# The transposes of both token tiles of an FFN chunk share one PSUM bank and are recorded in one loop

## The chip, the cores and the metric

The kernel runs on one NeuronCore of a Trainium2 chip. The metric is the device time of one execution in microseconds (us). A core has engines with queues of their own: TensorE (PE: matmuls and transposes; PEld: its weight loads, which overlap them), VectorE (DVE), ScalarE (ACT), GpSimd (POOL) and SyncE (SP, which issues the loads here). They run beside each other, each works its queue in order, and an instruction waits at the head of its queue until the semaphores that it names have been raised.

## The reference, cut to what matters

Two layers over 256 tokens of width 1024. Each layer is a feed-forward stage (FFN), a mixer (a state-space branch beside an attention branch) and a second FFN. Only the FFN is touched:

```
def swiglu(h, wi, wo):
    gate, up = jnp.split(h @ wi, 2, axis=-1)
    return (jax.nn.silu(gate) * up) @ wo

for l in range(DEPTH):
    x = x + 0.5 * swiglu(rms_norm(x, norm_ffn1[l]), ffn1_wi[l], ffn1_wo[l])
    ...                                     # the mixer
    x = x + 0.5 * swiglu(rms_norm(x, norm_ffn2[l]), ffn2_wi[l], ffn2_wo[l])
```

The inner width is 2816, so `wi` is 1024 x 5632 and `wo` 2816 x 1024.

## The kernel before

**Tiles.** The 256 tokens are two token tiles, t = 0 and 1, of 128. An FFN runs over 11 chunks c of 256 inner columns. In a chunk, `gemm` multiplies both tiles with 256 gate and 256 up columns of `wi` into two PSUM banks named `gu`. ACT computes the silu of the gate half (line 512), DVE multiplies it with the up half (line 513), which gives `act[t]`, 128 tokens x 256. To be multiplied with `wo` it has to stand with its inner columns on the partitions, so PE transposes it in two blocks of 128 x 128 (line 496) into a PSUM bank named `tr`, of which there are two, shared with all other transposes of the program.

**Split numbers.** Each product is formed from a high and a low part of both factors in three matmuls: line 381 (high x high), 382 (low of the first x high) and 383 (high x low), in `mm3`. So every factor has to be split: `split` (lines 347 to 349) copies the value to the short format on ACT (a cast, the high part) and then subtracts that from the value on DVE (the low part). Weights are split the same way when they have landed: `ffn_wi` and `w_in` with the gain of the norm on lines 169 (ACT, `whi`) and 170 (DVE, `wlo`), `ffn_wo` on line 349. There are four buffers of each for the split weights, so a weight split waits until PE has read the buffer for the last time.

**The product with `wo`** is formed one chunk late: `wo_mm(c - 1, t, i)` adds 128 inner columns of the chunk before to the PSUM banks `ya` (tile 0, two halves) and `yb` (tile 1). So in the loop stand: the matmuls of `gu` for chunk c, half of the `wo` matmuls for chunk c - 1, the transposes for chunk c, and the other half. At the last chunk no next one follows: `finish` (line 385 on) calls `part(0, 0)`, which multiplies the transposed tile 0 of that very chunk with `wo`, then the rest for tile 1. Behind `part(0, 0)` DVE adds the result to the residual `x` (line 391) and PE transposes `x` for the next stage (line 375).

**What sets the order.** The program is recorded in the order of the code, and a scheduler then gives each engine its queue, by a model of when operands are ready. `tc.issue_after(ins)` holds what is recorded in its block behind `ins`, for instructions of the same engine as `ins`. Tiles of a pool wait for the last reader of the buffer that they take. `k.bg` is side work of the mixer's preparation that is recorded between the chunks of the first FFN of each layer.

Of the kernel before, what the change touches and what calls it, by code (L numbers as in the profile page):

```python
# [11 lines left out]
ALU = mybir.AluOpType  # L12
# [67 lines left out]
class Model:  # L80
# [127 lines left out]
    def plan(k):  # L208
# [28 lines left out]
        for l in range(L):  # L237
            ffn(l, A['ffn1_wi'], A['ffn1_wo'], 0)
            cols(l, C_U)
            cols(l, C_KC, 384)  # L240
            cols(l, C_VS, 408)
            w1 = A['cmp_w1']
            for kv in range(2):
                for i in range(2):
                    k.add(bass.AP(tensor=w1.tensor, offset=w1.offset + ((l * 2 + kv) * 2048 + i * 1024) * 128,
                                  ap=[[128, 128], [128 * 128, 8], [1, 128]]), split=False)
            for c0 in (C_Q, C_GA, C_GA + 512, C_GB, C_GB + 512):
                cols(l, c0)
            for c in range(4):
                for i in range(2):  # L250
                    k.add(ap2(A['ssm_w_glu'], l, i * 256, 2, c * 256, D, 256))
            for c in range(2):
                for i in range(2):
                    w = A['nsa_w_up']
                    k.add(tuple(bass.AP(tensor=w.tensor, offset=w.offset + (l * 512 + g * 256 + i * 128) * D + c * 512,
                                        ap=[[D, 64], [64 * D, 2], [1, 512]]) for g in range(2)))
            for i in range(8):
                k.add(ap(A['w_out'], l, i * 128, 1, 0, D))
            ffn(l, A['ffn2_wi'], A['ffn2_wo'], 2)
# [219 lines left out]
    def ffn(k, hooks, sc, norm, order):  # L479
        nc = k.nc  # L480
        y = {}
        aT = {}

        def wo_mm(c, t, i, W, hs=(0, 1)):
            ah, al = aT[c, t]
            hi, lo = W
            for h in hs:
                cs = slice(h * 512, (h + 1) * 512)
                k.mm3(y[t, h], (ah[:, i], al[:, i]), (hi[:, cs], lo[:, cs]),
                      c == 0 and i == 0, c == NFF - 1 and i == 1)  # L490

        def transposes(c, act):
            for t in range(2):
                b = k.bank((128, 2, 128))
                for i in range(2):
                    nc.tensor.transpose(b[:, i], act[t][:, i * 128:(i + 1) * 128], k.id)  # L496
                hi = k.sb([128, 2, 128], "w1k", k.opt['n1'], F32R)
                lo = k.sb([128, 2, 128], "w1k", k.opt['n1'], F32R)
                k.split(b, hi, lo)
                aT[c, t] = (hi, lo)  # L500

        last = NFF - 1
        for c in range(NFF):
            ps = k.gemm(k.hstat, 8, 512, order if c == 0 else None, la=k.opt['LB'] if c == 0 else None)
            if c == 0:
                k.norms()
                r = k.rn
            act = []
            for t in range(2):
                sg = k.sb([128, 256], "w1k", k.opt['n1'])  # L510
                a = k.sb([128, 256], "w1k", k.opt['n1'])
                m = nc.scalar.activation(sg, ps[t][:, :256], AF.Silu, scale=r[t])  # L512
                nc.vector.scalar_tensor_tensor(a, ps[t][:, 256:], r[t], sg, op0=ALU.mult, op1=ALU.mult)  # L513
                act.append(a)
            if c == 0:
                k.fence, k.fence_n = (m,), k.opt['FB']
                k.prepare(k.opt['LA'])
                for t in range(2):
                    for h in range(2):
                        y[t, h] = k.bank((128, 512), 'yb' if t else 'ya')  # L520
                transposes(c, act)
            else:
                W = k.next()
                for t in range(2):
                    wo_mm(c - 1, t, 0, W)
                transposes(c, act)
                W = k.next()
                wo_mm(c - 1, 0, 1, W)
                if c < last:
                    wo_mm(c - 1, 1, 1, W)  # L530
            if c in hooks:
                hooks[c]()
        Ws = [k.next() for i in range(2)]

        def part(t, i0):
            for h in range(2):
                for i in range(i0, 2):
                    wo_mm(last, t, i, Ws[i], (h,))

        k.finish(y, sc, norm, (lambda: part(0, 0), lambda: wo_mm(last - 1, 1, 1, W), lambda: part(1, 0)))  # L540
# [893 lines left out]
```

## Time and profile before

| | |
|---|---|
| time, median of 3 runs | 1167.68 us (1165.56 to 1167.82) |
| time of the profiled execution | 1167.36 us |
| its span, first to last instruction | 1165.6 us |
| PE busy | 1153.3 us (99%) |
| DVE busy | 827.1 us (71%) |
| ACT busy | 671.9 us (58%) |
| mean granted TensorE clock | 0.997 |

A matmul's record holds its way through the array, so neighbours overlap: what a matmul costs is read from the distance of two starts. A row of the timeline that says x2 holds two instructions of the same kind behind each other. In the rows, `w1k` is a buffer of 1 KB per partition (the activation and its two parts), `hh` and `hl` are the parts of the normed input.

### The profile page before, as it was taken

How to read it: one execution, taken by the hardware profiler on the slowest of the kernel's cores; microseconds unless marked ns; L12 is line 12 of the kernel's file. 1: busy time of each engine (PE TensorE's matmuls, PEld its weight loads, DVE VectorE, ACT ScalarE, POOL GpSimd, SP SyncE). 2: the span in 40 equal slices, each digit the busy share in tenths (PEclk: the TensorE clock that was granted, in tenths of full speed). 3: DMA queues.
4: the chain of work that ended last, by engine and by line, in shares of the span. 5: the costliest groups of instructions: out<-in, count | busy, mean ns of one | idle time of the engine just before them, and what ended most of it. 6: DMA issues, size and time to landing. Idle time of an engine off the chain costs nothing.

```text
span 1165.6 us, 17595 instructions
## 1 busy us (share of the span) xinstructions
PE 1153.3 (99%) x6148; PEld 939.7 (81%) x6148; DVE 827.1 (71%) x1578; ACT 671.9 (58%) x1176; POOL 96.0 (8%) x177
## 2 busy tenths in 40 slices
PE   9999999999999999999999999999999999999998
PEld 6888887877877888888888888788788778888886
DVE  5798597797776665555567986977987666655654
ACT  6755665646674565555566565555667646555552
POOL 3000000021032000000030000002112200000000
PEclk9999999999999999999999999999999999999999
DMA  8765646464443566665665555565654335766662
GB/s 239 232 193 166 186 144 209 124 204 141 155 118 106 174 206 191 187 183 185 192 181 184 181 179 169 157 178 158 200 162 145 109 110 170 227 184 185 191 183 88
DMA packets 150266, 200.40 MB, mean 172 GB/s; under 512 B 10145, under 2 KB 121025, under 8 KB 150177
## 3 DMA queue, kind: packets, MB, share of 16 engines
q1 hardware_dynamic: 148656, 196.93, 55.4%
q0 software_dynamic: 1136, 1.82, 0.8%
q8 instruction: 48, 0.79, 0.3%
q10 hardware_dynamic: 384, 0.52, 0.2%
q14 instruction: 42, 0.34, 0.1%
HBM read 198.18 MB, written 1.05 MB: 171 GB/s over the span
## 4 chain that ended last, share of the span: by engine, by line
PE 95%; DVE 3%; ACT 1%; issue 0%; POOL 0%; DVEq 0%; ACTq 0%; POOLq 0%
PE gu L381 20%; PE gu L383 20%; PE gu L382 20%; PE yb L382 4%; PE yb L383 4%; PE yb L381 4%; PE ya L383 4%; PE ya L381 4%; PE ya L382 4%; PE tr L496 2%; PE yb L1238 1%; PE yb L907 1%; PE tr L375 1%; PE tr L1227 1%; PE gu L448 1%; PE ya L1194 1%
## 5 line engine op out<-in xcount | busy, mean ns | idle before, releaser
L169 ACT ACTIVATE whi<-raw,gcol 128x512 fp32r<-128x512 f32 (+2 forms) x480 | 316.2, 710 | 197.8 <-PE gu L382 84.7
L170 DVE SCALAR_TENSOR_TENSOR wlo<-raw,gcol,whi 128x512 fp32r<-128x512 f32 (+2 forms) x480 | 335.6, 738 | 108.2 <-ACT whi L169 106.2
L381 PE MATMUL gu<-whi,hh 128*128 128x512 f32 (+2 forms) x944 | 373.5, 396 | 1.8 <-ACT r L1322 1.8
L383 PE MATMUL gu<-wlo,hh 128*128 128x512 f32 (+2 forms) x944 | 367.7, 393 | 0.0
L382 PE MATMUL gu<-whi,hl 128*128 128x512 f32 (+2 forms) x944 | 367.6, 389 | 0.0
L349 DVE TENSOR_TENSOR wlo<-raw,whi 128x1024 fp32r<-128x1024 f32 x128 | 156.5, 1225 | 120.0 <-ACT whi L349 117.2
L381 PEld LDWEIGHTS gu<-whi,hh 128*128 128x128 f32 x944 | 177.9, 188 | 36.3 <-ACT r L1322 2.6
L382 PEld LDWEIGHTS gu<-whi,hl 128*128 128x128 f32 x944 | 178.1, 189 | 34.8 <-issue 0.2
L383 PEld LDWEIGHTS gu<-wlo,hh 128*128 128x128 f32 x944 | 177.3, 188 | 34.8 <-issue 0.3
L349 ACT CAST whi<-raw 128x1024 fp32r<-128x1024 f32 x128 | 134.4, 1053 | 121.2 <-PE gu L382 102.4
L382 PE MATMUL yb<-whi,w1k 128*128 128x512 f32 x176 | 71.2, 406 | 0.2
L382 PE MATMUL ya<-whi,w1k 128*128 128x512 f32 x176 | 68.7, 392 | 0.0
L383 PE MATMUL yb<-wlo,w1k 128*128 128x512 f32 x176 | 68.1, 392 | 0.0
L381 PE MATMUL yb<-whi,w1k 128*128 128x512 f32 x176 | 68.0, 393 | 0.0
L381 PE MATMUL ya<-whi,w1k 128*128 128x512 f32 x176 | 67.6, 394 | 0.0
L383 PE MATMUL ya<-wlo,w1k 128*128 128x512 f32 x176 | 67.1, 390 | 0.0
L349 ACT CAST w1k<-tr 128x256 fp32r<-128x256 f32 x88 | 32.4, 368 | 43.5 <-PE tr L496 43.1
L513 DVE SCALAR_TENSOR_TENSOR w1k<-gu,rs,w1k 128x256 f32<-128x256 f32 x88 | 42.0, 479 | 16.8 <-ACT w1k L512 16.8
L512 ACT ACTIVATE w1k<-gu,rs 128x256 f32<-128x256 f32 x88 | 40.9, 467 | 18.4 <-PE gu L383 15.7
L356 POOL TENSOR_SCALAR rs<-ss 128x1 f32<-128x1 f32 (+3 forms) x22 | 6.8, 309 | 523.8 <-ACT w2k L363 472.3
L1217 POOL TENSOR_SCALAR w2k<-w2k,sm 128x128 f32<-128x128 f32 (+1 forms) x64 | 35.1, 568 | 103.8 <-DVE sm L1209 48.6
L349 DVE TENSOR_TENSOR w1k<-tr,w1k 128x256 fp32r<-128x256 f32 x88 | 36.6, 419 | 9.9 <-ACT w1k L349 9.8
(316 smaller groups left out, 1378.9 us busy)
## 6 DMA issues: line engine op xcount, KB each, us to landing
raw<-in_ffn_wi_dram SPq DMA_DIRECT2D x352, 256.0 KB, 3.3
raw<-in_ffn_wo_dram SPq DMA_DIRECT2D x88, 512.0 KB, 3.6
raw<-in_w_in_dram SPq DMA_DIRECT2D x48, 512.0 KB, 4.5
raw<-in_ssm_w_glu_dram SPq DMA_DIRECT2D x32, 256.0 KB, 3.0
raw<-in_w_out_dram SPq DMA_DIRECT2D x16, 512.0 KB, 3.7
raw<-in_cmp_w_dram SPq DMA_DIRECT2D x8, 512.0 KB, 4.9
raw<-in_nsa_w_up_dram SPq DMA_DIRECT2D x16, 256.0 KB, 4.0
raw<-in_w_in_dram SPq DMA_DIRECT2D x8, 408.0 KB, 4.2
```

The lines of the kernel that those rows point to most:

```text
L169: k.hi_ins[i] = k.nc.scalar.activation(hi[:, s], r[:, s], AF.Copy, scale=c)
L170: k.lo_ins = k.nc.vector.scalar_tensor_tensor(lo[:, s], r[:, s], c, hi[:, s].bitcast(F32), op0=ALU.mult, op1=ALU.subtract)
L349: return k.nc.scalar.copy(hi, src), k.nc.vector.tensor_sub(lo, src, hi.bitcast(F32))
L375: m = k.nc.tensor.transpose(b[:, i], src[:, i * 128:(i + 1) * 128], k.id)
L381: mm(ps, a[0], b[0], start=first, stop=False)
L382: mm(ps, a[1], b[0], start=False, stop=False)
L383: return mm(ps, a[0], b[1], start=False, stop=last)
L448: last[2] = k.nc.tensor.matmul(ps[t], stat(kk, t)[a], W[i][b][:, cs[j]], start=kk == 0 and a + b == 0 and j == 0, stop=kk == nk - 1 and (a ...
L496: nc.tensor.transpose(b[:, i], act[t][:, i * 128:(i + 1) * 128], k.id)
L512: m = nc.scalar.activation(sg, ps[t][:, :256], AF.Silu, scale=r[t])
L513: nc.vector.scalar_tensor_tensor(a, ps[t][:, 256:], r[t], sg, op0=ALU.mult, op1=ALU.mult)
L1217: G.tensor_scalar(w[:, i], p[:, i], cf[:, j:j + 1], 0.0, op0=ALU.mult, op1=ALU.add)
```

## The change

The two transposes of tile 0 and the two of tile 1 go into four quarters of one bank (128 x 2 x 2 x 128 values, a whole bank), recorded in one loop ahead of both splits, in an `issue_after` block that names the second tile's product on line 513, an instruction of DVE (`k.act_ins` is written twice, the second tile's last). Each split then reads its half of the bank. Line 496 is 498 now, and lines behind it are three higher (512 is 515, 907 is 910).

```diff
         def transposes(c, act):
+
+            b = k.bank((128, 2, 2, 128))
+            with k.tc.issue_after(k.act_ins.ins):
+                for t in range(2):
+                    for i in range(2):
+                        nc.tensor.transpose(b[:, t, i], act[t][:, i * 128:(i + 1) * 128], k.id)
             for t in range(2):
-                b = k.bank((128, 2, 128))
-                for i in range(2):
-                    nc.tensor.transpose(b[:, i], act[t][:, i * 128:(i + 1) * 128], k.id)
                 hi = k.sb([128, 2, 128], "w1k", k.opt['n1'], F32R)
                 lo = k.sb([128, 2, 128], "w1k", k.opt['n1'], F32R)
-                k.split(b, hi, lo)
+                k.split(b[:, t], hi, lo)
                 aT[c, t] = (hi, lo)
...
-                nc.vector.scalar_tensor_tensor(a, ps[t][:, 256:], r[t], sg, op0=ALU.mult, op1=ALU.mult)
+                k.act_ins = nc.vector.scalar_tensor_tensor(a, ps[t][:, 256:], r[t], sg, op0=ALU.mult, op1=ALU.mult)
```

The first place is PE's queue at the end of the second FFN of layer 0, from the transposes of the last chunk on; `yb` are matmuls of tile 1 for the chunk before, `ya` the first ones that need the transposed tile 0. Before:

```order
L496 MATMUL tr_5804<-id_68,w1k_5778 128x128 [waits DVE_49]
L496 MATMUL tr_5804<-id_68,w1k_5778 128x128
L382 MATMUL yb_4386<-whi_5761,w1k_5675 128x512
L383 MATMUL yb_4386<-wlo_5762,w1k_5674 128x512
L381 MATMUL yb_4387<-whi_5761,w1k_5674 128x512
L382 MATMUL yb_4387<-whi_5761,w1k_5675 128x512
L383 MATMUL yb_4387<-wlo_5762,w1k_5674 128x512
L496 MATMUL tr_5811<-id_68,w1k_5782 128x128 [waits DVE_49,PE_49]
L496 MATMUL tr_5811<-id_68,w1k_5782 128x128
L381 MATMUL ya_4384<-whi_5788,w1k_5807 128x512 [waits Activation_49]
L381 MATMUL ya_4385<-whi_5788,w1k_5807 128x512
L382 MATMUL ya_4384<-whi_5788,w1k_5808 128x512 [waits DVE_49]
```

The same stretch with the change:

```order
L498 MATMUL tr_5783<-id_68,w1k_5757 128x128 [waits DVE_49]
L498 MATMUL tr_5783<-id_68,w1k_5757 128x128
L382 MATMUL yb_4375<-whi_5740,w1k_5654 128x512
L383 MATMUL yb_4375<-wlo_5741,w1k_5653 128x512
L381 MATMUL yb_4376<-whi_5740,w1k_5653 128x512
L382 MATMUL yb_4376<-whi_5740,w1k_5654 128x512
L383 MATMUL yb_4376<-wlo_5741,w1k_5653 128x512
L498 MATMUL tr_5783<-id_68,w1k_5761 128x128 [waits DVE_49]
L498 MATMUL tr_5783<-id_68,w1k_5761 128x128
L381 MATMUL ya_4373<-whi_5767,w1k_5788 128x512 [waits Activation_49]
L381 MATMUL ya_4374<-whi_5767,w1k_5788 128x512
L382 MATMUL ya_4373<-whi_5767,w1k_5789 128x512 [waits DVE_49]
```

PE's order is the same in both; the two pairs stand apart still, and what differs is the bank (`tr_5804` and `tr_5811` before, `tr_5783` for both now).

The second place is ACT's queue over the same stretch: `whi` on line 169 are weight splits for the next stage, `w1k<-tr` on line 349 are the casts of the two transposed tiles, `hh` belongs to the next stage. Before:

```order
L169 ACTIVATE whi_5834<-raw_5758,gcol_102 128x512 [waits DMAHW0_49,DMAHW1_49,DVE_49,PE_49]
L169 ACTIVATE whi_5834<-raw_5758,gcol_102 128x512
L349 CAST w1k_5807<-tr_5804 128x256 [waits PE_49]
L169 ACTIVATE whi_5843<-raw_5785,gcol_102 128x512 [waits DMAHW2_49,DMAHW3_49,DVE_49,PE_49]
L169 ACTIVATE whi_5843<-raw_5785,gcol_102 128x512
L349 CAST w1k_5814<-tr_5811 128x256 [waits DVE_49,PE_49]
```

With the change:

```order
L169 ACTIVATE whi_5812<-raw_5737,gcol_102 128x512 [waits DMAHW0_49,DMAHW1_49,DVE_49,PE_49]
L169 ACTIVATE whi_5812<-raw_5737,gcol_102 128x512
L169 ACTIVATE whi_5821<-raw_5764,gcol_102 128x512 [waits DMAHW2_49,DMAHW3_49,DVE_49,PE_49]
L169 ACTIVATE whi_5821<-raw_5764,gcol_102 128x512
L349 CAST w1k_5788<-tr_5783 128x256 [waits PE_49]
L349 CAST w1k_5792<-tr_5783 128x256 [waits DVE_49]
```

The first tile's cast has gone behind the second pair of weight splits, and the second tile's cast names DVE alone: in the built program that is the first tile's subtraction. DVE's queue mirrors this: `wlo` on line 170 twice, then both subtractions. The same holds at the end of the first FFN of either layer; at the last FFN's end the two casts follow each other without weight splits, before as now.

The third place is PE's queue in the mixer of layer 1, behind the small matmuls of line 550 (553 now): line 907 (910 now) needs what DVE computes on line 936, and `gu` are large matmuls. Before:

```order
L550 MATMUL ya_8435<-kc2_7587,raw_8286 64x33 x15
L907 MATMUL yb_8761<-r8_7271,r4_8056 64x128 [waits DVE_49,PE_49]
L907 MATMUL yb_8761<-r8_7271,r4_8056 64x128
L907 MATMUL yb_8761<-r8_7350,r4_8522 64x128 [waits DVE_49]
L907 MATMUL yb_8761<-r8_7350,r4_8522 64x128
```

With the change:

```order
L553 MATMUL ya_8402<-kc2_7556,raw_8253 64x33 x15
L381 MATMUL gu_8477<-whi_8405,hh_86 128x512 [waits PE_49,Activation_49]
L382 MATMUL gu_8477<-whi_8405,hl_87 128x512
L381 MATMUL gu_8478<-whi_8405,hh_86 128x512 [waits PE_49]
L382 MATMUL gu_8478<-whi_8405,hl_87 128x512
L910 MATMUL yb_8728<-r8_7242,r4_8023 64x128 [waits DVE_49]
L910 MATMUL yb_8728<-r8_7242,r4_8023 64x128
L910 MATMUL yb_8728<-r8_7321,r4_8489 64x128 [waits DVE_49]
```

Four large matmuls have come ahead of line 907.

## Rows read from the trace of the kernel before

**Rows 1.** Page, busy time of the engines, share of the span, instructions

```profile
PE 1153.3 (99%) x6148; PEld 939.7 (81%) x6148; DVE 827.1 (71%) x1578; ACT 671.9 (58%) x1176; POOL 96.0 (8%) x177
```

**Rows 2.** Windows inside two FFNs (window, length, busy of each engine, PEclk, DMA, GB/s)

```profile
20.00:195.00 175.00, 174.91 (x865) 142.47 (x866) 144.34 (x348) 103.83 (x166) 12.71 (x19) 1.00 0.63 189
400.00:575.00 175.00, 175.00 (x789) 143.23 (x788) 102.12 (x148) 96.89 (x151) 1.80 (x4) 1.00 0.61 187
```

**Rows 3.** Waits of PE, whole program (waited for: total us, times, longest us)

```profile
PE yb L907 <- DVE r L936: 3.1, 2, 1.5
PE gu L381 <- ACT r L1322: 1.8, 2, 1.3
```

**Rows 4.** Timeline of PE, FFN end at 580 us (start us, us, instruction)

```profile
580.25 0.38 PE L496 MATMUL tr<-id,w1k 128*128 128x128 f32 x2
580.39 0.71 PE L381 MATMUL ya<-whi,w1k 128*128 128x512 f32 x2
...
580.93 0.39 PE L382 MATMUL ya<-whi,w1k 128*128 128x512 f32 x1
```

**Rows 5.** Timeline of ACT, same end

```profile
579.28 0.37 ACT L349 CAST w1k<-tr 128x256 fp32r<-128x256 f32 x1 [0.69 <-PE tr L496]
580.22 1.34 ACT L169 ACTIVATE whi<-raw,gcol 128x512 fp32r<-128x512 f32 x2 [0.56 <-PE yb L382]
581.46 0.35 ACT L349 CAST w1k<-tr 128x256 fp32r<-128x256 f32 x1
```

**Rows 6.** Timeline of DVE, same end

```profile
580.98 1.42 DVE L170 SCALAR_TENSOR_TENSOR wlo<-raw,gcol,whi 128x512 fp32r<-128x512 f32 x2 [0.86 <-ACT whi L169]
582.31 0.42 DVE L349 TENSOR_TENSOR w1k<-tr,w1k 128x256 fp32r<-128x256 f32 x1
```

**Rows 7.** Timelines of PE and DVE, FFN ends at 198 and 776 us

```profile
199.28 0.40 PE L382 MATMUL ya<-whi,w1k 128*128 128x512 f32 x1
200.66 0.42 DVE L349 TENSOR_TENSOR w1k<-tr,w1k 128x256 fp32r<-128x256 f32 x1
...
777.32 0.40 PE L382 MATMUL ya<-whi,w1k 128*128 128x512 f32 x1
778.69 0.42 DVE L349 TENSOR_TENSOR w1k<-tr,w1k 128x256 fp32r<-128x256 f32 x1
```

**Rows 8.** Timelines of PE, ACT and DVE, last FFN end

```profile
1155.63 0.71 PE L381 MATMUL ya<-whi,w1k 128*128 128x512 f32 x2
1155.91 0.37 ACT L349 CAST w1k<-tr 128x256 fp32r<-128x256 f32 x1 [1.01 <-PE tr L496]
...
1156.18 0.39 PE L382 MATMUL ya<-whi,w1k 128*128 128x512 f32 x1
1156.32 0.42 DVE L349 TENSOR_TENSOR w1k<-tr,w1k 128x256 fp32r<-128x256 f32 x1 [0.96 <-ACT w1k L349]
```

**Rows 9.** Timeline in the mixer of layer 1, ACT and PE

```profile
882.04 0.67 ACT L1322 ACTIVATE r<-gu,rh 128x512 f32<-128x512 f32 x1
...
882.77 0.50 PE L381 MATMUL gu<-whi,hh 128*128 128x512 f32 x1
...
883.11 0.39 PE L382 MATMUL gu<-whi,hl 128*128 128x512 f32 x1
```

**Rows 10.** Timeline of ACT, a chunk inside an FFN

```profile
1004.55 0.38 ACT L349 CAST w1k<-tr 128x256 fp32r<-128x256 f32 x1 [0.26 <-PE tr L496]
1005.94 1.05 ACT L349 CAST whi<-raw 128x1024 fp32r<-128x1024 f32 x1 [1.01 <-PE gu L382]
```

**Rows 11.** Windows in the mixer of layer 0, then PE's timeline there

```profile
243.00:251.00 8.00, 6.32 (x92) 4.70 (x90) 7.74 (x20) 5.09 (x9) 1.99 (x2) 0.79 0.80 264
276.00:280.00 4.00, 2.73 (x13) 1.93 (x12) 4.00 (x8) 3.89 (x8) 0.00 (x0) 1.00 0.83 224
...
249.28 0.63 PE L381 MATMUL gu<-whi,hh 128*128 128x512 f32 x1
249.70 0.63 PE L382 MATMUL gu<-whi,hl 128*128 128x512 f32 x1
```

## The prediction

> **What bounds the kernel now.** I read the page's busy times first: TensorE (PE) is busy for 1153.3 us of the 1165.6 us span [rows 1], so the time is that of PE's queue, and an edit counts only where it makes PE wait or takes a wait from it. Next the windows: inside the feed-forward stages PE is busy for 175.00 of 175.00 us (second FFN of layer 0) and 174.91 of 175.00 us (first FFN of layer 0) [rows 2]. There is no wait in there that an edit of the FFN could remove. Then the waits of PE: the two large ones are 3.1 us in two waits for VectorE (DVE) at line 936 and 1.8 us in two for ScalarE (ACT) at line 1322 [rows 3]; both lines belong to the mixer, not to the FFN. So nearly nothing is to be won at the transposes. What is left is to ask what they can lose, and that is read in the timeline at the four places where an FFN ends: there the result of the transposes is needed at once.
>
> **What the change does to the program.** It says that the four transposes are issued in one stretch behind the second activation. The order of instructions shows otherwise: in 40 of the 44 chunks they still stand as two pairs, with 5 to 20 matmuls between, since the helper orders only what is recorded on the engine of the instruction it is given (DVE), and transposes are PE's. What does change is that both pairs write one bank. The first split's cast therefore waits for the fourth transpose, the second cast for the first split's subtraction, and the scheduler has moved the first cast and its subtraction behind one more pair of weight splits (lines 169 and 170).
>
> **The price, part by part.** No instruction is added or removed: 4 FFNs of 11 chunks with 4 transposes, 2 casts and 2 subtractions each, before and after. The DMA queue keeps its order.
>
> *Inside a chunk: nothing.* After the transposes come 15 to 43 matmuls of the next chunk before their result is used, 3.4 us at the least (15 x 0.23 us; 789 starts in 175.00 us are 0.22 us each, with the shorter transposes among them [rows 2], and I take 0.23 for a full matmul). In the chunk at 1004 us the second cast starts at 1004.55 us and the next weight cast at 1005.94 us, when PE lets go of its buffer [rows 10]. With the change that slot holds cast, subtraction, cast: 0.38 + 0.42 [rows 6] + 0.38 + two handoffs of 0.06 us [rows 9], to 1005.85 us. It fits, barely; ACT's idle time hides it. If that cover is gone (first FFN of each layer, where DVE is fuller), the weight splits slip by some tenths; PE is full there now [rows 2], so I take 0 and keep up to +2 us for the range.
>
> *Three FFN ends with weight splits in the queue (198, 580, 776 us).* Take 580 us. Now the second pair of transposes starts at 580.25 us, the two matmuls that need the first tile's cast at 580.39 us and the first one that needs its subtraction at 580.93 us, without a wait [rows 4]. The cast ran at 579.28 us, ahead of the weight splits of 580.22 us; the cast of the second tile came behind them, 581.46 to 581.81 us [rows 5]. In the new order the first tile's cast has that place, so it is there at 581.81 us. DVE likewise: behind its weight pair (580.98 us for 1.42) stands now the second tile's subtraction, 582.31 to 582.73 us [rows 6]; the first tile's takes its place. The weight splits wait for PE's matmuls ahead of the transposes, which haven't moved, so these places hold. From the end of a cast to the matmul that waited for it I read 0.06 us (882.71 to 882.77), and the matmul after a wait takes 0.34 us to the next instead of 0.23, its weights not loaded ahead: 0.11 us [rows 9]. So the matmul of 580.93 us starts at 582.73 + 0.06 = 582.79 us, 1.86 us late, and 0.11 us more is lost behind it: 1.97 us. The wait for the cast (581.87 against 580.39) lies inside that. At 198 us: 200.66 + 0.42 + 0.06 - 199.28 = 1.86, with 0.11 it is 1.97 us; at 776 us: 778.69 + 0.42 + 0.06 - 777.32 = 1.85, so 1.96 us [rows 7]. Behind the waiting matmul stand twelve of the tile's output, the residual update that waits for these, and the transposes for the next stage: all move along, nothing catches up. Three ends: 5.90 us.
>
> *The last end (1155 us)* has no weights left to split. The first cast takes the place of the second: 1155.91 + 0.37 + 0.06 = 1156.34 us for the two matmuls of 1155.63 us [rows 8]. They take 0.34 + 0.23 us, so the third starts at 1156.91 us, behind the subtraction's end (1156.32 + 0.42 + 0.06 = 1156.80), instead of at 1156.18 us: 0.73 us.
>
> The trace bears on one point of this: before, the two pairs lie in two banks, and each cast starts once its own pair is done (579.28 and 1155.91 us) [rows 5, 8]. The Trainium skill, page "PSUM — Partial Sum Buffer", section "PSUM bank collisions raise a hardware error", says that two engines must not be in one bank at once even at different columns, so waits go by bank. By that rule the sum stands as it is; if columns alone counted, the last end would cost nothing and the sum would be 0.73 us smaller. No run here shows such a collision.
>
> *The mixer.* The scheduler's order there differs too, though the work is the same. One difference can be priced: in layer 1 four matmuls now stand ahead of the matmuls of line 907, where PE waited for DVE (half of the 3.1 us [rows 3]); they fill 4 x 0.23 = 0.92 us of it. In layer 0 the same wait stands as before. The rest is bounded by what reordering did already: from the end of its first FFN to the end of its second, layer 0 takes 580.93 - 199.28 = 381.65 us and layer 1 takes 1156.18 - 777.32 = 378.86 us for the same work [rows 4, 7, 8]. So another order is worth up to 2.8 us either way; I take -0.92 us.
>
> Sum: 5.90 + 0.73 - 0.92 = 5.71 us. The profiled execution took 1167.36 us for its span of 1165.6 us, 0.32 us below the median of 1167.68 us. I predict 1167.36 + 5.71 = 1173.1 us.
>
> **Rivals.** *Not slower: the mixer gives it back.* The place is line 907 and the two waits for line 1322. The most it can give is PE's 4.9 us of waits [rows 3] and the two stretches in which the granted clock fell: 0.79 over the 8 us at 243 us, that is 3.4 us at the lower of the two levels, 1.2 GHz, where matmuls start 0.42 us apart instead of 0.23 (249.28 and 249.70 us), some 8 x 0.19 = 1.5 us each [rows 11]. Together 7.9 us, which would end at 1167.36 + 6.63 - 7.9 = 1166.1 us. It decides from 4.3 us given back (6.63 - 2.3). For it: all this hangs on places in the queue, and the order there is new. Against it: DVE's order ahead of line 936 is the same in both programs, and in layer 0 PE's, too.
>
> *The clock falls at the new waits.* At 243 us it fell after a stretch of small matmuls and a wait of about 1.5 us; at 276 us, after a wait of 1.3 us among full matmuls, it stayed at 1.00 [rows 3, 11]. The new waits are of 1.5 us, among full matmuls, so I give this little. Three falls would cost 3 x 1.5 = 4.6 us: 1177.7 us.
>
> *DVE in the first FFNs.* There DVE is busy for 144.34 of 175 us against 102.12 in the second FFN [rows 2], and ACT now waits for DVE's subtraction before its second cast; weight splits could come late for PE. Up to 2 us in each layer: 1177 us. Against it: PE shows no wait for weights there now.
>
> *The freed bank helps the side work of layer start (other transposes take banks from the same two).* PE has no wait in the FFN to give up [rows 2], so this is worth 0 and gets no chance of its own.
>
> **How the numbers follow.** The forecast gets 0.68, with a range of its own of 1170.5 to 1175.5 us (the mixer's 2.8 us either way, less the part that I already count); the mixer's give-back 0.13; the clock 0.12; late weights 0.07. No change is what a measurement cannot tell from it, 0.2% or 2.3 us. The give-back splits into 0.09 for within that and 0.04 for faster; all else is slower, 0.87. The range from 1169.5 to 1177.0 us leaves out most of the give-back and the upper half of the clock's case.
>
> **What would show it.** Right: PE waits of about 1.5 us for ACT at line 349 (two matmuls of `ya`), then 0.4 us for DVE, at three FFN ends, and 0.7 us at the last; the interiors of the FFNs full as before, chunk by chunk; the first cast behind the weight pair. Wrong: no waits there, or PE waits inside the chunks, or a mixer that is more than 3 us longer or shorter.

## The result and the profile after

The changed kernel takes 1174.42 us (median of 6 runs, 1173.29 to 1175.68) against 1167.38 us (median of 6, 1165.49 to 1167.82): 7.0 us more, a ratio of 1.0067 (1.0057 to 1.0077). The profiled execution took 1174.3 us with a span of 1172.5 us, 6.9 us more than before. The forecast was 1173.1 us.

The page's busy times of the kernel after hardly differ from [rows 1]: the work is the same, and what came is waiting.

```profile
PE 1153.7 (98%) x6148; PEld 940.4 (80%) x6148; DVE 828.9 (71%) x1578; ACT 670.7 (57%) x1176; POOL 94.3 (8%) x177
```

The waits of PE after (waited for: total us, times, longest us), which answer to [rows 3]:

```profile
PE ya L381 <- ACT w1k L349: 4.2, 4, 1.2
PE yb L382 <- DVE w1k L349: 2.6, 3, 1.1
PE gu L381 <- ACT whi L169: 1.7, 1, 1.7
PE yb L910 <- DVE r L939: 1.5, 1, 1.5
PE tr L375 <- DVE x L391: 1.0, 3, 0.3
PE ya L382 <- DVE w1k L349: 0.5, 3, 0.2
PE tr L498 <- DVE w1k L516: 0.5, 1, 0.5
```

The first line and the sixth are the four FFN ends that were forecast. The second and the last lie inside the first FFNs, where none was. The third is new in the mixer of layer 1. The fifth, at the transposes of the residual behind an end, costs nothing by itself: at 580 us it is 1.60 us from the last matmul of `ya` to the first of `yb` after, and 1.58 before. Of the 3.1 us at line 907 (910 now) half has gone, and the 1.8 us at line 1322 (1325 now) are gone.

The FFN end of [rows 4] in PE's timeline after (start us, us, instruction; in brackets idle time before it and who ended it):

```profile
580.95 0.38 PE L498 MATMUL tr<-id,w1k 128*128 128x128 f32 x2
582.57 0.73 PE L381 MATMUL ya<-whi,w1k 128*128 128x512 f32 x2 [1.23 <-ACT w1k L349]
583.48 0.50 PE L382 MATMUL ya<-whi,w1k 128*128 128x512 f32 x1 [0.18 <-DVE w1k L349]
583.82 0.39 PE L383 MATMUL ya<-wlo,w1k 128*128 128x512 f32 x1
```

and ACT's beside it, which answers to [rows 5]:

```profile
580.92 1.33 ACT L169 ACTIVATE whi<-raw,gcol 128x512 fp32r<-128x512 f32 x2 [1.63 <-PE yb L382]
582.16 0.35 ACT L349 CAST w1k<-tr 128x256 fp32r<-128x256 f32 x1
583.46 0.37 ACT L349 CAST w1k<-tr 128x256 fp32r<-128x256 f32 x1 [0.95 <-DVE w1k L349]
```

and DVE's, to [rows 6]:

```profile
581.68 1.42 DVE L170 SCALAR_TENSOR_TENSOR wlo<-raw,gcol,whi 128x512 fp32r<-128x512 f32 x2 [1.55 <-ACT whi L169]
583.01 0.42 DVE L349 TENSOR_TENSOR w1k<-tr,w1k 128x256 fp32r<-128x256 f32 x1
```

Read them across: the second pair of transposes starts at 580.95 us, but ACT has gone into the weight splits at 580.92 us and casts only at 582.16 us; PE waits 1.23 us for that. DVE subtracts behind its own weight splits, to 583.43 us, and PE starts 0.05 us later. From the second pair to that matmul it is 2.53 us against 0.68 us in [rows 4], 1.85 us more; 1.86 was forecast. The second cast starts 0.03 us after the first subtraction has ended, though it reads the other half of the bank. The Trainium skill, page "PSUM — Partial Sum Buffer", section "PSUM bank collisions raise a hardware error", has the guard by bank and not by column. This trace agrees; but the wait is one that the built program names, so no run shows what would come without it.

The last end, which answers to [rows 8], is the bank's wait alone, since no weights are split there:

```profile
1161.79 0.38 PE L498 MATMUL tr<-id,w1k 128*128 128x128 f32 x2
1162.63 0.73 PE L381 MATMUL ya<-whi,w1k 128*128 128x512 f32 x2 [0.46 <-ACT w1k L349]
1163.20 0.40 PE L382 MATMUL ya<-whi,w1k 128*128 128x512 f32 x1
```

The windows after (length, busy of each engine, PEclk, DMA, GB/s) show a hole in the first FFN of layer 0 (first row; 174.91 of 175 us before [rows 2]) and none in the second (second row):

```profile
20.00:195.00 175.00, 173.22 (x856) 140.90 (x856) 143.62 (x347) 102.70 (x164) 12.96 (x19) 1.00 0.62 186
400.00:575.00 175.00, 175.00 (x789) 143.17 (x789) 101.91 (x149) 97.11 (x151) 1.80 (x4) 1.00 0.61 188
```

One of the three waits in there, PE's timeline after:

```profile
163.20 0.50 PE L382 MATMUL yb<-whi,w1k 128*128 128x512 f32 x1 [1.15 <-DVE w1k L349]
```

and DVE's queue ahead of it after (the last row is the second tile's subtraction):

```profile
159.58 0.69 DVE L593 TENSOR_TENSOR w2k<-s5q,w2k 128x512 f32<-128x512 f32 x1
160.19 0.74 DVE L170 SCALAR_TENSOR_TENSOR wlo<-raw,gcol,whi 128x512 fp32r<-128x512 f32 x1
160.86 0.69 DVE L595 TENSOR_TENSOR w2k<-s5q,w2k 128x512 f32<-128x512 f32 x1
161.46 0.68 DVE L600 TENSOR_TENSOR w2k<-s5q,w2k 128x512 f32<-128x512 f32 x1
162.06 0.74 DVE L170 SCALAR_TENSOR_TENSOR wlo<-raw,gcol,whi 128x512 fp32r<-128x512 f32 x1
162.72 0.42 DVE L349 TENSOR_TENSOR w1k<-tr,w1k 128x256 fp32r<-128x256 f32 x1
```

The same stretch of DVE before, where the subtraction follows its weight split at once:

```profile
160.00 0.69 DVE L590 TENSOR_TENSOR w2k<-s5q,w2k 128x512 f32<-128x512 f32 x1
160.61 0.74 DVE L170 SCALAR_TENSOR_TENSOR wlo<-raw,gcol,whi 128x512 fp32r<-128x512 f32 x1
161.28 0.41 DVE L349 TENSOR_TENSOR w1k<-tr,w1k 128x256 fp32r<-128x256 f32 x1
161.61 0.68 DVE L592 TENSOR_TENSOR w2k<-s5q,w2k 128x512 f32<-128x512 f32 x1
```

Two pieces of the mixer's side work (lines 595 and 600, 592 and 597 before) have come ahead of it, 0.6 us each; the weight split next to it stood ahead of it before, too. Its own cast, in ACT's timeline after, had long ended, at 157.51 us, so it is the place in the queue that is late, not the operand:

```profile
157.16 0.35 ACT L349 CAST w1k<-tr 128x256 fp32r<-128x256 f32 x1
```

To compare whole programs I cut PE's starts at the transposes: an FFN from the fourth transpose of its first chunk to the fourth of its last; the end from there to the first matmul of the next stage (of the last FFN: to the last matmul); the mixer from there to the fourth transpose of the next FFN's first chunk. In us, from one trace each:

| kernel | FFN 1, 2 of layer 0 | FFN 1, 2 of layer 1 | the four ends | mixer, layer 0, 1 |
|---|---|---|---|---|
| before | 175.65, 168.08 | 175.72, 168.08 | 7.07, 7.05, 7.05, 5.34 | 206.50, 203.73 |
| after | 177.70, 168.08 | 176.93, 168.08 | 9.02, 9.03, 9.02, 6.11 | 202.89, 204.16 |
| ends | 175.66, 168.08 | 175.69, 168.08 | 9.03, 9.03, 9.02, 6.09 | 203.38, 203.20 |
| inner | 177.66, 168.08 | 176.94, 168.08 | 7.05, 7.04, 7.05, 5.34 | 204.98, 204.06 |
| forced | 177.75, 168.08 | 176.90, 168.08 | 7.78, 7.80, 7.78, 6.09 | 206.56, 203.10 |
| hold | 177.04, 167.47 | 176.99, 167.47 | 8.80, 8.80, 8.79, 6.12 | 205.33, 203.18 |
| subfirst | 177.11, 168.08 | 176.09, 167.98 | 9.00, 9.04, 9.03, 6.09 | 206.53, 203.37 |
| joinb | 175.53, 167.46 | 175.54, 167.49 | 7.04, 7.05, 7.05, 5.36 | 204.95, 203.75 |
| joina | 182.06, 167.47 | 182.11, 167.47 | 7.07, 7.05, 7.05, 5.36 | 205.38, 206.53 |

After against before: the ends +6.67, the first FFNs +3.26, the second ones 0.00, the mixers -3.18, the start +0.31: together +7.06 us (the span is 6.9 us longer, as what follows the last matmul is 0.14 us shorter).

### The profile page after: what moved, and what is told of

Same layout as the page of the kernel before. It is cut to its first block, busy times and chain, and to the rows that moved or that the text cites. A ratio compares the mean times of both kernels' runs of the same rounds, so it can differ in the third digit from the quotient of the medians.

```text
span 1172.5 us, 17554 instructions
## 1 busy us (share of the span) xinstructions
PE 1153.7 (98%) x6148; PEld 940.4 (80%) x6148; DVE 828.9 (71%) x1578; ACT 670.7 (57%) x1176; POOL 94.3 (8%) x177
## 5 line engine op out<-in xcount | busy, mean ns | idle before, releaser
L381 PEld LDWEIGHTS ya<-whi,w1k 128*128 128x128 f32 x176 | 32.7, 188 | 11.9 <-ACT w1k L349 5.1
```

The lines of the kernel that those rows point to most:

```text
L381: mm(ps, a[0], b[0], start=first, stop=False)
```

## The experiments

Each ratio is to the kernel before as it ran beside that version: a median of 1166.12 us (11 runs) for ends, inner, forced and hold, of 1167.08 us (15 runs) for subfirst, joinb and joina. The expectations start from 1167.4 or 1166.8 us.

**ends and inner: one half of the change each.**

```diff
+            if c == NFF - 1:        # ends;  c < NFF - 1 in inner
                 b = k.bank((128, 2, 2, 128))
                 ...
+            else:
+                for t in range(2):
+                    b = k.bank((128, 2, 128))
                     ...
```

> Shared bank at the last chunk of each FFN alone; all other chunks keep two banks. Theory (the bank makes the first cast late, and that counts where an FFN ends): the four ends cost as in the changed kernel, from the second pair of transposes to the next stage's first matmul 9.14 us instead of 7.16 at three of them and 0.73 us at the last, 6.6 us together; the first FFNs' interiors run as before (177.4 us from first to last transpose), with no wait for the second tile's subtraction. The mixers' order lies between the two kernels, worth 0 to -3.6 us. So 1167.4 + 6.6 - 1.5 = 1172.5 us (1170.4 to 1174.0). Rival (the cost is spread over all 44 chunks, 7.0/44 = 0.16 us each): 1167.4 + 0.6 = 1168.0 us, and the ends stay at 7.2 us.

Measured: 1170.70 us, a ratio of 1.0041 (1.0028 to 1.0053). The four ends are those of the changed kernel to 0.02 us, the first FFNs those of before.

> Shared bank in chunks 0 to 9 of each FFN; the last chunk keeps two banks. Theory: the ends go back to 7.16 us and the casts alternate with the weight splits as before; the first FFNs keep the waits for the second tile's subtraction (179.4 and 178.6 us from first to last transpose, +2.05 and +1.20); the second FFNs stay at 169.81 us; the mixers' order is almost that of before, so 0 +- 1 us. 1167.4 + 3.25 = 1170.6 us (1169.6 to 1171.6). Rival (cost spread over the chunks): 40/44 of 7.0 us, 1173.8 us.

Measured: 1169.00 us, 1.0026 (1.0015 to 1.0037), 0.6 us under the range given; against the kernel before beside it, it is 2.9 us more where 3.2 us were forecast. The ends are those of before, the first FFNs those of the changed kernel. PE's waits in inner hold the interior's lines and none of `ya` for ACT:

```profile
PE yb L382 <- DVE w1k L349: 2.5, 3, 1.1
PE tr L499 <- DVE w1k L526: 0.5, 1, 0.5
```

So the two costs are apart: 6.67 us belong to the last chunk, 3.26 us to the others, and these only in the first FFN of a layer. A cost spread evenly over the chunks is ruled out. (Neither the loop nor the hold has a part in it: built with two banks and all four transposes recorded ahead of the splits, the program has the order of before on every engine, and without the hold on line 513's product it is the changed program itself. So neither was run.) Both kernels come in lower than their parts because of the mixers (last column), more on which below.

**forced: the first cast ahead of the weight splits, the bank still shared.** The second pair of weight splits at an end is held behind the first tile's cast, which puts ACT's and DVE's queues there in the order of before.

```diff
-                k.split(b[:, t], hi, lo)
+                k.cast[t] = k.split(b[:, t], hi, lo)[0]
...
-        Ws = [k.next() for i in range(2)]
+        Ws = [k.next()]
+        if norm:
+            k.fence, k.fence_n = (k.cast[0],), 1
+        Ws.append(k.next())
```

> The changed kernel, but at the end of an FFN (not the last one) the second pair of weight splits is held behind the first tile's cast, so that cast and weight splits stand as before; the bank stays shared. Theory (of the 1.97 us at each of three ends 0.73 us is the wait for the fourth transpose and 1.24 us the place behind the weight splits): from the second pair of transposes to the next stage's first matmul 7.16 + 0.73 = 7.9 us, and the first FFNs' interiors as in the changed kernel (+3.25 us). With the mixers as before: 1167.4 + 4 x 0.73 + 3.25 = 1173.6 us, with the mixer of layer 0 as in the changed kernel 1170.0. Rival (the place is harmless, the bank's wait is all of it): 9.14 us at the ends, 1177.3 us with the mixers as before.

Measured: 1172.61 us, 1.0059 (1.0046 to 1.0072). PE's timeline in forced (lines are one higher there):

```profile
583.29 0.38 PE L499 MATMUL tr<-id,w1k 128*128 128x128 f32 x2
584.13 0.73 PE L382 MATMUL ya<-whi,w1k 128*128 128x512 f32 x2 [0.46 <-ACT w1k L350]
584.70 0.40 PE L383 MATMUL ya<-whi,w1k 128*128 128x512 f32 x1
```

and ACT's:

```profile
583.70 0.37 ACT L350 CAST w1k<-tr 128x256 fp32r<-128x256 f32 x1 [2.08 <-PE tr L499]
583.97 1.34 ACT L170 ACTIVATE whi<-raw,gcol 128x512 fp32r<-128x512 f32 x2
585.21 0.36 ACT L350 CAST w1k<-tr 128x256 fp32r<-128x256 f32 x1
```

The cast goes first, the wait is 0.46 us as at the last end, and the three ends take 7.79 us: 0.73 us over before, 1.24 us under the changed kernel. Of the 1.97 us, then, 0.73 is the bank's wait and 1.24 the place behind the weight splits. The rival, by which the place is harmless, is out.

**hold: four transposes in one stretch.** The second tile's pair is recorded first and the first tile's held behind it, so all 44 chunks have what the change says.

```diff
-            with k.tc.issue_after(k.act_ins.ins):
-                for t in range(2):
-                    for i in range(2):
-                        nc.tensor.transpose(b[:, t, i], act[t][:, i * 128:(i + 1) * 128], k.id)
+            for i in range(2):
+                m = nc.tensor.transpose(b[:, 1, i], act[1][:, i * 128:(i + 1) * 128], k.id)
+            with k.tc.issue_after(m.ins):
+                for i in range(2):
+                    nc.tensor.transpose(b[:, 0, i], act[0][:, i * 128:(i + 1) * 128], k.id)
```

> What the change says: all four transposes of a chunk stand in one stretch behind the second activation (the second tile's pair is recorded first, the first tile's is held behind it), one bank. Theory (the first cast waits for the fourth transpose anyway, and transposes cost PE the same apart or together: a pair 0.22 us, four 0.44): the ends stay at 9.14 us, the second FFNs at 169.8 us, the first FFNs within 1 us of the changed kernel's; 1174.4 us (1173 to 1176). Rival (joined transposes save a turn between short and long matmuls, 0.09 us in each of 44 chunks, which is what the change was to bring): 1174.4 - 4.0 = 1170.4 us and the second FFNs 169.8 - 0.9 = 168.9 us.

Measured: 1173.35 us, 1.0063 (1.0049 to 1.0077). The stretch in PE's timeline:

```profile
414.26 0.38 PE L496 MATMUL tr<-id,w1k 128*128 128x128 f32 x2
414.48 0.38 PE L499 MATMUL tr<-id,w1k 128*128 128x128 f32 x2
414.62 0.48 PE L381 MATMUL gu<-whi,hh 128*128 128x512 f32 x1
414.94 0.39 PE L382 MATMUL gu<-whi,hl 128*128 128x512 f32 x1
```

Neither theory had the size. The second FFNs go from 168.08 to 167.47 us over ten chunks, 0.06 us a chunk, where one said 0 and the other 0.09. The first matmul behind a transpose still takes 0.32 us to the next (414.62 to 414.94), once a chunk now instead of twice, but the transposes in a row have their distance of 0.108 us more often, which takes nearly all of that back. What is left is small and spread: the second to ninth matmul behind a stretch take 0.230 us to the next on average (0.231 before, and half as many of them now), those further off 0.2281 us (0.2286 before). The ends still take 8.80 us at three of them, against 7.05 before, and the first FFNs 1.39 and 1.27 us more than before, though only one of the waits for the second tile's subtraction is left there (1.1 us) beside one for the product of the activation (1.2 us). So the stretch repays little of what the shared bank costs.

**subfirst: the side work behind the second tile's subtraction.**

```diff
-                k.split(b[:, t], hi, lo)
+                k.sub = k.split(b[:, t], hi, lo)[1]
...
-        k.pull()
+        with ExitStack() as e:
+            if k.sub is not None:
+                e.enter_context(k.tc.issue_after(k.sub.ins))
+            k.pull()
```

> The changed kernel, with the side work of the first FFNs held, on DVE, behind the second tile's subtraction of the chunk recorded before it. Theory (the three new waits of 2.6 us inside the first FFNs come from that subtraction's place behind side work in DVE's queue): those waits go and the first FFNs take 175.7 us from the first chunk's last transpose to the last chunk's, as before the change, instead of 177.7 and 176.9; the ends stay at 9.03 us. With the mixer of layer 0 ordered as before the change (its order here is nearly that) the total is 1174.4 - 3.2 + 3 = 1174 us; with the changed kernel's mixers 1171. Rival (DVE has no room there at all, so what is moved ahead makes the weight splits late): the first FFNs stay near 177 us, with PE's waits at lines 169 and 170 instead.

Measured: 1175.30 us, 1.0073 (1.0059 to 1.0086). The waits for that subtraction are gone, but others stand in their place, for the product of the activation (line 520 here, once in either first FFN) and in the side work's own transposes (line 832, in layer 0):

```profile
PE tr L502 <- DVE w1k L520: 1.5, 2, 0.8
PE tr L832 <- ACT r L833: 0.8, 1, 0.8
```

The first FFNs gain 0.59 and 0.84 us of the 2.05 and 1.21; the total is higher than the changed kernel's because the mixer of layer 0 takes 206.53 us again. The first theory is right on where the waits came from and wrong that putting the subtraction ahead is enough; the rival is right that something else then comes late, and named the wrong victim.

**joinb and joina: the stretch with two banks.** Chunks 0 to 9 are recorded as in hold, but with a bank for each pair; the last chunk is as before. In the second FFNs PE's trace has all ten stretches of four; in the first ones of joinb the pairs of chunks 5 to 7 stand apart still, with 8, 8 and 21 matmuls between. The two versions differ in which split is recorded first.

```diff
-            b = k.bank((128, 2, 2, 128))
+            bs = [k.bank((128, 2, 128)) for t in range(2)]
             ...
-            for t in range(2):
+            for t in (1, 0):        # joinb;  (0, 1) in joina
                 ...
-                k.split(b[:, t], hi, lo)
+                k.split(bs[t], hi, lo)
```

> Two banks as before the change; in chunks 0 to 9 of each FFN the four transposes stand in one stretch behind the second activation (second tile's pair first, its split first too), the last chunk as before. PE's order in both mixers is that of before. Theory (a stretch of four costs PE less than two pairs, by 0.06 us a chunk, as the kernel with the held stretch showed: 167.47 instead of 168.08 us over ten chunks of a second FFN): 40 x 0.06 = 2.4 us less, 1166.8 - 2.4 = 1164.4 us, if the first FFNs get no wait for the second tile's subtraction. Rival 1 (that 0.6 us was something else of that kernel, the transposes' place is worth nothing): 168.08 us stay, 1166.8 us. Rival 2 (the first tile's cast, now later, makes waits in the first FFNs): 177 us there, 1167 to 1169 us.

Measured: 1165.64 us (11 runs, 1164.19 to 1166.29), 0.9987 (0.9978 to 0.9996) of the kernel before: the one version here that takes less than the kernel before, by about 1.4 us, where 2.4 were forecast. The second FFNs gain 0.62 and 0.59 us as forecast; the first ones only 0.12 and 0.18, less than seven stretches at 0.06 us would give, and what takes the rest is not shown. PE has no waits in FFNs; these lines, of the mixers, are those of [rows 3]:

```profile
PE yb L921 <- DVE r L950: 3.1, 2, 1.5
PE gu L381 <- ACT r L1336: 1.8, 2, 1.3
```

> As joinb, but the first tile's split stands first. Theory: the second FFNs as in joinb, 167.5 us; in the first FFNs the second tile's subtraction comes later in DVE's queue than in joinb, so waits for it may show, up to 1 us each. The mixers' order is another one (layer 0 differs much, layer 1 less), worth 0 to -3.6 us by the runs so far: 1164.4 - 1.5 + 1 = 1164 us (1161 to 1166). Rival (other orders of the mixer are as often worse as better): 1165 to 1168 us.

Measured: 1180.37 us, 1.0118 (1.0103 to 1.0132), a plain miss. With the first tile's split recorded first, its subtraction stands behind side work in both first FFNs:

```profile
PE ya L382 <- DVE w1k L349: 7.3, 2, 3.6
PE ya L381 <- ACT w1k L349: 2.1, 2, 1.1
```

They take 182.1 us instead of 175.5. The clock makes it worse: behind the wait of 3.64 us, which ends at 164.09 us, the matmuls start 0.43 us apart, the distance of 1.2 GHz, and the granted clock (third number from the end) is 0.57 over 4 us:

```profile
164.00:168.00 4.00, 3.92 (x10) 3.10 (x11) 4.00 (x9) 0.00 (x0) 0.00 (x0) 0.57 0.50 131
```

The order in which two splits are recorded is worth 6.5 us an FFN here, the clock's part included, because it sets a place in the queue of an engine that is busy for more than 80% of the time there.

## Why the prediction was right, and where it was not

**The FFN ends: right, in place and size.** Forecast 5.90 + 0.73 = 6.63 us, measured 6.67. The parts hold as well: ends has them alone, inner has none, forced takes out the 1.24 us of the place and leaves the 0.73 us of the bank at each of three ends.

**"Inside a chunk: nothing": wrong for the first FFNs.** The second FFNs did stay at 168.08 us, ACT's slot held. In the first FFNs I took 0, with up to +2 us kept for the range and up to 2 us a layer in a rival; measured are +2.05 and +1.21. The size was foreseen, the reason was not: not the weight splits came late for PE but the second tile's subtraction, which now stands behind side work of the mixer (and once, in layer 1, the product of the activation, 0.5 us). That the scheduler put it there because it expected the cast later is my reading; no run shows its model. [rows 2] had warned (DVE busy 144.34 of 175 us); what I did not do was compare DVE's order there, chunk by chunk, as I did at the ends.

**The mixers: the sign right, the size and the place wrong.** Forecast -0.92 us in layer 1, measured -3.61 us in layer 0 and +0.43 in layer 1. The four matmuls that now stand ahead of line 910 in layer 1 wait themselves, for weights; PE's timeline after:

```profile
824.80 3.93 PE L553 MATMUL ya<-kc,raw 128*64 128x33 f32 x128
830.47 0.79 PE L381 MATMUL gu<-whi,hh 128*128 128x512 f32 x1 [1.74 <-ACT whi L169]
```

I priced what they would fill and not what they need. The clock has a part in it as well: behind that new wait it stays low for longer than behind the old one. Over 8 us there the granted clock is 0.57 after (first row) and 0.79 before (second row), by which the lower level lasts about 6.9 us instead of 3.4:

```profile
829.00:837.00 8.00, 6.54 (x24) 4.74 (x25) 7.74 (x20) 5.94 (x10) 1.99 (x2) 0.57 0.61 198
824.00:832.00 8.00, 7.34 (x41) 5.75 (x42) 7.74 (x20) 7.26 (x13) 1.99 (x2) 0.79 0.77 239
```

From start to start, without the waits, the matmuls of `gu` (512 columns, `hh` and `hl`) take 1.3 us more in this mixer than before; its other places gave about 0.9 us back. That this is near the forecast's 0.92 us is luck too: the wait to be filled was 1.55 us, and the one that came in its place is 1.74. In layer 0 the 1.8 us at line 1322 went, which I had only as part of a rival; the rest of its 3.61 us I can bound but not explain. By PE's starts 1.4 us of it lie in the attention's small matmuls and transposes (lines 1230 and 1241 now), 13.3 us instead of 14.7; I made no run on the mixers alone.

So one term was 3.26 us too low and another 2.26 us too high; with the start (+0.31) and the ends (+0.04) the sum came out 1.35 us low. The ends were forecast rightly; that the total is so near is luck beyond that, as two errors cancel.

**The rivals.** *The mixer gives it back*: it gave 3.18 of the 4.3 us from which it would have decided; with the interiors it was not near. *The clock falls at the new waits*: no matmul behind the four ends starts 0.42 us apart, so there it did not in the profiled execution; where it did last longer is the mixer of layer 1, behind a wait that was not forecast. *DVE in the first FFNs*: in its effect this came true, 3.26 of the up to 4 us, on top of the forecast, with another instruction than the one it named. *The freed bank*: no term of the table shows a gain from it.

## What to carry to other kernels

Where two pieces of work went into one PSUM bank here, the first consumer waited for the last writer and the readers on two engines took turns. Look for the place where that result is needed at once (here the last chunk, 0.73 us), since in the steady state it may cost nothing at all (here the second FFNs, 168.08 us either way). When a scheduler orders the queues, a dependency that is later in its model also moves its instructions behind others, and that can cost more than the wait (here 1.24 us an end): compare the order on every engine that is nearly full, not only at the exposed places. Price a moved instruction by what it waits for in its new place as well as by the hole that it fills.

## What the runs showed of the hardware

The same order of PE takes two times in the mixer of layer 0, with the granted clock as the only difference that I found. The windows there, of before:

```profile
240.00:256.00 16.00, 14.32 (x195) 11.21 (x194) 15.74 (x31) 10.32 (x21) 3.90 (x5) 0.89 0.67 203
```

and of joinb, whose order of PE is the same:

```profile
240.00:256.00 16.00, 14.33 (x202) 11.44 (x201) 15.74 (x31) 10.56 (x22) 4.04 (x5) 1.00 0.67 204
```

With the fall that mixer takes 206.50, 206.56 and 206.53 us (before, forced, subfirst), without it 204.98 and 204.95 us (inner, joinb); PE's order in that mixer is the same in all five. That is 1.55 us for one fall, close to the 1.5 us of the prediction. It comes in some of these executions and not in others, behind the same wait of 1.5 us. The price is that of one place: in layer 1 PE's order of before takes 203.73 and 203.75 us with a fall (before, joinb) and 203.20 us without (ends), which waits 0.6 us longer there for another reason.

Single runs of one program differ as well. The 11 runs of joinb stand in two groups: five with a mean granted clock of 0.998 or more at 1164.19 to 1164.82 us, six with 0.996 or 0.997 at 1165.64 to 1166.29 us. Most of the five have 0.999 and most of the six 0.996; 0.003 of 1163 us is about 7 us at the lower level, two falls like the one above rather than one, and which they were no trace shows. The six runs of the changed kernel go from 0.998 at 1173.29 us to 0.993 at 1175.68 us. So a difference of 1 to 2 us between two single profiles of this program says nothing before the clock in the mixers has been compared.
